# Value rows turned on their way to DRAM, first weights in halves, and a planner that counts the issuing queue as busy

## Chip, core and metric

One core of a Trainium2 chip. The metric is the device time of one execution in microseconds (us). TensorE is called PE, VectorE DVE, ScalarE ACT, GpSimd POOL and SyncE SP. Nearly all transfers are issued by SP, in the order of its instructions.

## The reference, cut to what matters

One encoder layer over 512 tokens of 1024 features, in float32:

```python
proj = h @ w_in                                  # queries, keys and values of two mixers, A and B
o_a = windowed_gqa_sink(rope(qa), rope(ka), va)  # 16 query heads, 4 key heads, |i-j| <= 128, blocks of 128
o_b = dilated_mixture(rope(qb), rope(kb), vb)    # 3 groups of 4 heads, dilation 1, 4, 16
g_a, g_b = split(sigmoid(h @ w_gate + b_gate))
y = (g_a * (o_a @ w_br_a) + g_b * (o_b @ w_br_b)) @ w_out
h = layer_norm(ALPHA * h + y)
f = (silu(h @ w_ff_gate) * (h @ w_ff_up)) @ w_ff_down
h = layer_norm(ALPHA * h + f)
```

## The kernel before

**Products.** Tokens stand in the order of four residues: token 4i + r is row i of residue r. Every float32 operand is split into a high part h and a low part l (a cast, then a subtraction), and a product is made of three: high by high, high by low, low by high. A *unit* of weights is 128 x 1024, loaded in two halves of 128 x 512 (256 KB); a half needs a staging slot ("ws", six of them) and two slots for its parts ("whl", sixteen). Lines 454 to 456 make the three products of one block of 128 features (`feat_k`), line 354 and line 333 the split of weights, and line 627 to 629 the values.

**The first units.** The first three units are `k`, `q` and `r` (keys of two heads, and queries). Their first halves come in two pieces, of `CUTS`, so that PE can begin early; `half_unit_by` loads, casts and subtracts each piece (lines 374 to 384). The eight blocks of x come from line 427, with the cast of line 429 and the subtraction of line 430. `FIRST` holds the priorities of these loads. Then, for each of the eight blocks, PE makes the three products of k, those of q and those of r.

**The order.** `ORDER` lists the work of the token mixers: `q2` is a unit of queries, `VA` the values of A and of B's first group, `T` a rotation of the heads gathered so far (rows are moved together by small transfers at line 483, turned on DVE, and moved back at line 504), `G` a gate unit, `A0` the attention of a group of heads in four blocks (`unit_a`), `B0` a head of mixer B (`unit_b`).

**The planner.** All operations are gathered with reads, writes and a priority: the PE time counted so far, plus an offset (-130 for weight loads and their splits, `EV` = -100 for what follows a product, `LATER` = 30). `Program.run` then goes through the operations with costs for each engine, picks for each free engine the ready operation of the lowest priority, and writes the instructions in this order. So the order on each engine is fixed when the program is built, and an engine waits where an operation in its list is not ready, whatever stands behind it. For SP, the planner counts an issue as 0.06 us and lets a backlog of issues grow beside it (`dma[0]`): a transfer that is ready is accepted at once.

**The values.** `token_values(False)` makes the values of A (256 columns) and of B's first group (256 columns) for the four residues. They are wanted by blocks of neighbouring tokens, so that rows have to be permuted: each residue's 128 x 512 is copied out of the accumulator and written to DRAM as it stands (line 639, one transfer of 256 KB). When all four are there, four transfers read A's blocks (line 645), 32 rows of each of the four residues, and eight read B's, shifted by half a block, 16 rows of each residue (line 651). `value_split` then makes a high and a low part of each block and group (a cast by line 333 or 335, a subtraction by line 589). The planner adds `READ` = 4 us to such a read.

**Where values are needed.** `unit_a` makes scores (lines 576, 577), exponentials on ACT (line 730), scaled probabilities (line 666 on ACT, 668 on DVE), transposes on PE (line 678) and then the products with the values (lines 743, 744).

Of the kernel before, what the change touches and what calls it, by code (L numbers as in the profile page):

```python
# [57 lines left out]
D_BANK = "s"  # L58
SPIN = 4

CUTS = ((0, 128), (128, 512))
FIRST = {("k", 0): (-1000, -998.3), ("q", 0): (-999.7, -998.1), ("r", 0): (-999.6, -998),
         ("k", 1): (-997.5,), ("q", 1): (-997.3,), ("r", 1): (-997.2,),
         "x": (-999.9, -998.4, -997.9, -997.8, -997.4, -997, -996.9, -996.8)}
N_WS, N_WHL, N_ATT, N_WHL1, N_TWO = 6, 16, 16, 40, 4


# [4 lines left out]


ORDER = """
q2 VA T G q3 A0 q4 G k1 T A1 q5 G q6 q7 T A2 G G A3
Q00 K00 T V Q02 K02 T Q01 K01 T B0 B1 G g Q10 K10 T g Q12 K12 T Q11 K11 T B2 B3 g8
"""

# [19 lines left out]
class Program:  # L98
# [72 lines left out]
    def run(self):  # L171
        engines = (PE, ACT, DVE, POOL, SP)
        free = {e: 0.0 for e in engines}
        pending = {e: [] for e in engines}
        times = [0.0]
        frees = []
        dma = [0.0, 0.0]

        def add(o):
            heapq.heappush(times, o.ready)  # L180
            for e, _ in o.alts:
                pending[e].append(o)

        seen = set()
        self.line, self.weights, self.loads = deque(), deque(), deque()
        for o in self.ops:
            new = [b for b in o.bufs if "gen" in b.keys and b not in seen]
            if new:
                seen.update(new)
                self.line.append(o)  # L190
            if o.strict and any("ws" in b.keys and b not in seen for b in o.bufs):
                seen.update(o.bufs)
                self.loads.append(o)
            if o.strict and any("whl" in b.keys and b not in seen for b in o.bufs):
                seen.update(o.bufs)
                self.weights.append(o)
            if o.left == 0:
                add(o)
        n_left = len(self.ops)
        while n_left:  # L200
            if not times:
                self.stuck(pending)
            now = heapq.heappop(times)
            while times and times[0] <= now:
                heapq.heappop(times)
            while frees and frees[0][0] <= now:
                _, _, b = heapq.heappop(frees)
                for key in b.keys:
                    if key in self.limits:
                        self.used[key] -= 1  # L210
            progress = True
            while progress:
                progress = False
                for e in engines:
                    if free[e] > now:
                        continue
                    best = None
                    for o in pending[e]:
                        if o.ready <= now and (best is None or o.prio < best.prio) and self.fits(o):
                            if e == DVE and len(o.alts) > 1 and free[ACT] < now + BIAS:  # L220
                                continue
                            best = o
                    if best is None:
                        continue
                    o = best
                    cost = dict(o.alts)[e]
                    if not o.urgent and any(q.urgent and now < q.ready < now + cost and q.prio < o.prio
                                            for q in pending[e]):
                        continue
                    for a, _ in o.alts:  # L230
                        pending[a].remove(o)
                    for b in o.bufs:
                        if b.tile is None:
                            b.tile = b.make()
                            for key in b.keys:
                                if key in self.limits:
                                    self.used[key] += 1
                    o.fn(e)
                    o.eng = e
                    if e == SP:  # L240
                        end = now + 0.06
                        dma[0] = max(dma[0], now) + (0.45 if cost > 0.2 else 0.62)
                        dma[1] = max(dma[1], dma[0] + 0.65) + cost
                        o.done = dma[1] + 0.9 + o.moves
                    elif o.moves:
                        end = now + cost
                        dma[1] = max(dma[1], end) + o.moves
                        o.done = dma[1] + 2.0
                    else:
                        end = now + cost  # L250
                        o.done = end
                    free[e] = end
                    heapq.heappush(times, end)
                    for b in o.bufs:
                        b.users -= 1
                        b.end = max(b.end, o.done)
                        if b.users == 0:
                            heapq.heappush(frees, (b.end + HOP, id(b), b))
                            heapq.heappush(times, b.end + HOP)
                    for q in o.succ:  # L260
                        same = len(q.alts) == 1 and q.alts[0][0] == e and e != SP and not o.moves
                        hop = SAME * (e in (ACT, DVE)) if same else HOP_PE if q.alts[0][0] == PE else HOP
                        q.ready = max(q.ready, o.done + hop)
                        q.left -= 1
                        if q.left == 0:
                            add(q)
                    n_left -= 1
                    progress = True
# [15 lines left out]
def pe(n):  # L284
    return max(0.11, 0.0133 + n / 2400)
# [3 lines left out]
def hybrid_layer(ctx: ExitStack, tc: tile.TileContext, wpack, xT, xtok, sink, bgate,  # L289
# [174 lines left out]
        for k in range(KD):  # L464
            feat_k(ps, wu, k, XM, xtok_of)

    EV, NOW, LATER, READ = -100.0, -300.0, 30.0, 4.0


    SHUF = [*range(8, 16), *range(0, 8), *range(24, 32), *range(16, 24)]  # L470
# [126 lines left out]
    def token_values(dilated):  # L597
# [22 lines left out]
        for r in range(NR):  # L620
            ps = bank("dense")
            for k in range(KD):
                wh, wl = parts_[k]

                def go(e, ps=ps, k=k, wh=wh, wl=wl, r=r):
                    a, b = xh[k]()[:, r * P:(r + 1) * P], xl[k]()[:, r * P:(r + 1) * P]
                    mm(ps.t, a, wh.t, start=(k == 0), stop=False)
                    mm(ps.t, a, wl.t, start=False, stop=False)
                    mm(ps.t, b, wh.t, start=False, stop=(k == KD - 1))

                op([(PE, 3 * pe(S))], go, reads=[wh, wl, *xtok_of(k)], writes=[ps])
                pr.T += 3 * pe(S)
            if dilated:
                for g in range(2):
                    res[g].append(value_split(ps, 256 * g, [ps]))
            else:
                t = slot()
                op(cp_alts(S, True), lambda e, t=t, ps=ps: copy(e, t.t, ps.t), reads=[ps], writes=[t], prio=EV)
                op([(SP, 0.73)], lambda e, t=t, r=r: nc.sync.dma_start(aside.t[r], t.t), reads=[t], writes=[(aside, r)],
                   prio=EV)  # L640
        if not dilated:
            raw = [slot() for _ in range(NR)]
            every = [(aside, r) for r in range(NR)]
            for m, t in enumerate(raw):
                op([(SP, 0.6)], lambda e, t=t, m=m: nc.sync.dma_start(
                    t.t[:, 0:256], aside.t[:, 32 * m:32 * m + 32, 0:256]), reads=every, writes=[(t, 0)], prio=EV, moves=READ)

            for m, t in enumerate(raw):
                for h in range(2):
                    c = 16 * ((2 * m - 1 + h) % 8)  # L650
                    op([(SP, 0.75)], lambda e, t=t, h=h, c=c: nc.sync.dma_start(
                        t.t[64 * h:64 * h + 64, 256:512], aside.t[:, c:c + 16, 256:512]), reads=every, writes=[(t, 1, h)],
                       prio=LATER, moves=READ)
            for g in range(2):
                for m, t in enumerate(raw):
                    res[g].append(value_split(t, 256 * g, [(t, 1, h) for h in range(2)] if g else [(t, 0)],
                                              LATER if g else EV))
        return res


# [277 lines left out]

    psk, psq, psr = bank("dense"), bank("dense"), bank("dense")
    for k in range(KD):  # L940
        for w, ps in (("k", psk), ("q", psq), ("r", psr)):
            feat_k(ps, [first[w, 0], first[w, 1]], k, XM, xtok_of)
    env = {"gate": 0, "qs": {}, "ks": {}, "turn": Turn()}
    ka = env["turn"].add(psk, k_post, 4)
    qa = env["turn"].add(psq, q_post, 4, (0, 0)) + env["turn"].add(psr, q_post, 4, (0, 0))
# [652 lines left out]
```

## Time and profile before

| | |
|---|---|
| median of 3 runs | 783.96 us (783.23 to 784.75) |
| profiled execution | 784.13 us, of which the span of instructions is 782.3 us |
| granted clock of PE | 0.996 |
| instructions | 13384, of which 4470 are products and as many weight loads |
| DMA | 113.36 MB, mean 145 GB/s |

The span is the time from the first to the last instruction; the rest of the profiled execution's time lies around it. A row of the timeline gives start, duration, engine, line, operation, output and input, shape and count; in square brackets stands how long the engine had been idle and what ended that. SPq rows are transfers at the moment at which SP issues them, not when they land. A PE row's duration reaches into the next one, since products are pipelined: the distance of two starts tells the pace.

### The profile page before, as it was taken

Reading aid. Unit: us, or ns where it says so; the run is one execution under the profiler, and the core shown is the slowest. Engines: PE = TensorE matmul, PEld = TensorE weight load, DVE = VectorE, ACT = ScalarE, POOL = GpSimd, SP = SyncE. Lnnn points to the kernel's source line nnn. Section 1 sums busy time; section 2 is a strip of 40 time slices with the busy share of each in tenths; the row PEclk is TensorE's granted clock in tenths of the full one; section 3 lists DMA queues with packets and bytes.
Section 4 is the critical chain, followed back from the end, with each engine's and each line's share of the span. In section 5 each row is a group of like instructions: output and inputs, shape, how many; then the busy total and the mean of one; then the engine's idle time right before and its main releaser. Section 6 shows DMA issues by size and latency. Waiting matters only on the chain.

```text
span 782.3 us, 13384 instructions
## 1 busy us (share of the span) xinstructions
PE 768.7 (98%) x4470; PEld 675.3 (86%) x4470; DVE 648.1 (83%) x1363; ACT 483.3 (62%) x1067; POOL 126.3 (16%) x288
## 2 busy tenths in 40 slices
PE   9998999999999999999999999999999999999995
PEld 5876888888888888888888899999999999999985
DVE  5486899888899899697687999888888889888697
ACT  5355796877688778693352667555665566555631
POOL 0010100101003503400011020142102330123002
PEclk9999999999999999999999999999999999999998
DMA  8745222312123324254373388689867986789202
GB/s 259 225 133 173 97 82 63 120 51 95 61 83 95 114 74 155 92 192 148 122 229 67 94 234 228 160 176 206 229 186 162 234 191 198 182 215 209 53 1 108
DMA packets 68789, 113.36 MB, mean 145 GB/s; under 512 B 8560, under 2 KB 17008, under 8 KB 68720
## 3 DMA queue, kind: packets, MB, share of 16 engines
q1 hardware_dynamic: 57056, 91.47, 36.1%
q0 software_dynamic: 11520, 20.98, 16.4%
q8 instruction: 35, 0.57, 0.3%
q14 instruction: 34, 0.28, 0.1%
q10 hardware_dynamic: 144, 0.07, 0.0%
HBM read 104.87 MB, written 4.72 MB: 140 GB/s over the span
## 4 chain that ended last, share of the span: by engine, by line
PE 89%; DMA 2%; DVE 1%; SPq 1%; issue 0%; ACT 0%; DVEq 0%; ACTq 0%
PE ps L454 10%; PE ps L455 10%; PE ps L456 10%; PE ps L1312 9%; PE ps L1311 9%; PE ps L1310 9%; PE ps L1439 4%; PE ps L1440 4%; PE ps L1441 4%; PE ps L1077 3%; PE ps L1076 3%; PE ps L1075 3%; PE ps L678 3%; PE ps L577 1%; PE ps L576 1%; PE ps L744 1%
## 5 line engine op out<-in xcount | busy, mean ns | idle before, releaser
L333 ACT ACTIVATE sl<-sl 128x512 fp32r<-128x512 f32 (+4 forms) x452 | 245.4, 570 | 87.7 <-PE ps L455 24.0
L1194 DVE TENSOR_TENSOR sl<-sl,sl 128x512 fp32r<-128x512 f32 (+3 forms) x304 | 169.9, 603 | 11.5 <-ACT sl L333 7.6
L333 ACT ACTIVATE sl<-ps 128x256 f32<-128x256 f32 (+4 forms) x204 | 89.4, 455 | 105.5 <-PE ps L1312 67.0
L454 PE MATMUL ps<-x,sl 128*128 128x512 f32 x304 | 121.4, 399 | 1.1 <-ACT sl L333 0.9
L455 PE MATMUL ps<-x,sl 128*128 128x512 f32 x304 | 119.3, 392 | 0.3 <-DVE x L430 0.2
L456 PE MATMUL ps<-x,sl 128*128 128x512 f32 x304 | 118.9, 391 | 0.4 <-DVE sl L354 0.4
L1264 POOL DMA_DIRECT2D sl<-wpack x44 | 40.4, 995 | 264.8 <-ACT sl L333 136.0
L354 DVE TENSOR_TENSOR sl<-sl,sl 128x512 fp32r<-128x512 f32 x114 | 75.7, 687 | 8.9 <-ACT sl L333 8.1
L1310 PE MATMUL ps<-x,sl 128*128 128x256 f32 x264 | 74.8, 283 | 0.0
L1312 PE MATMUL ps<-x,sl 128*128 128x256 f32 x264 | 74.7, 283 | 0.0
L1311 PE MATMUL ps<-x,sl 128*128 128x256 f32 x264 | 74.7, 283 | 0.0
L456 PEld LDWEIGHTS ps<-x,sl 128*128 128x128 f32 x304 | 57.1, 188 | 13.5 <-DVE sl L354 0.8
L1194 DVE TENSOR_TENSOR sl<-sl,ps 128x512 f32<-128x512 f32 (+1 forms) x78 | 47.4, 611 | 25.5 <-PE ps L1312 16.6
L454 PEld LDWEIGHTS ps<-x,sl 128*128 128x128 f32 x304 | 57.3, 189 | 11.9 <-ACT sl L333 2.2
L455 PEld LDWEIGHTS ps<-x,sl 128*128 128x128 f32 x304 | 57.3, 188 | 10.2 <-DVE x L430 1.2
L1311 PEld LDWEIGHTS ps<-x,sl 128*128 128x128 f32 x264 | 50.6, 192 | 0.5
L1310 PEld LDWEIGHTS ps<-x,sl 128*128 128x128 f32 x264 | 50.6, 192 | 0.5
L1312 PEld LDWEIGHTS ps<-x,sl 128*128 128x128 f32 x264 | 50.6, 192 | 0.0
L1312 PE MATMUL ps<-tw,sl 128*128 128x256 f32 x176 | 49.8, 283 | 0.0
L1311 PE MATMUL ps<-tw,sl 128*128 128x256 f32 x176 | 49.8, 283 | 0.0
L1312 PE MATMUL ps<-sl,sl 128*128 128x256 f32 x176 | 49.8, 283 | 0.0
L1310 PE MATMUL ps<-tw,sl 128*128 128x256 f32 x176 | 49.8, 283 | 0.0
(150 smaller groups left out, 1860.9 us busy)
## 6 DMA issues: line engine op xcount, KB each, us to landing
sl<-wpack SPq DMA_DIRECT2D x235, 256.0 KB
sl<-wpack POOLq DMA_DIRECT2D x44, 256.0 KB, 5.4
wf<-wpack SPq DMA_DIRECT2D x36, 256.0 KB
wf<-wpack POOLq DMA_DIRECT2D x36, 256.0 KB, 6.5
sl<-sl SPq DMA_DIRECT2D x88, 32.0 KB
sl<-xT SPq DMA_DIRECT2D x8, 256.0 KB
sl<-wpack SPq DMA_DIRECT2D x16, 128.0 KB
sl<-xtok SPq DMA_DIRECT2D x8, 256.0 KB
```

The costliest lines, as they stand in the source:

```text
L333: nc.scalar.activation(dst, src, AF.Copy)
L354: op([(DVE, dve(S))], lambda e: nc.vector.tensor_tensor(l.t, src.t, f32(h.t), op=ALU.subtract), reads=[src, h], writes=[l], prio=prio, abs ...
L454: mm(o, a, x0, start=(k == 0), stop=False)
L455: mm(o, a, x1, start=False, stop=False)
L456: mm(o, b, x0, start=False, stop=(k == nk - 1))
L1194: op([(DVE, dve(w))], lambda e: nc.vector.tensor_tensor(dst(), x(), y(), op=o), reads=reads, writes=writes, prio=prio)
L1264: return op([(POOL, 1.0)], lambda e: nc.gpsimd.dma_start(dst.t, wpack[u, :, j * S:(j + 1) * S], accum_op=ALU.add), reads=[dst], writes=[ds ...
L1310: mm(o, wh, bh[k](), start=(first and k == 0), stop=False, skip_group_check=True)
L1311: mm(o, wh, bl[k](), start=False, stop=False, skip_group_check=True)
L1312: mm(o, wl, bh[k](), start=False, stop=(k == 3), skip_group_check=True)
L1439: mm(ps.t, x0, w[0].t, start=(first and m == 0), stop=False, skip_group_check=True)
L1440: mm(ps.t, x0, w[1].t, start=False, stop=False, skip_group_check=True)
```

## The change

1. The first halves of k, q and r are cut into 256 and 256 columns instead of 128 and 384, and the priorities are set anew, so that x blocks 2 and 3 come ahead of some of the second pieces.
2. For each of the first six blocks, PE makes the products by parts: high by high for k, q and r, then low weight by high x for all three, then high weight by low x. For the last two blocks it finishes one unit after the other, in the same order of parts.
3. In `ORDER`, `k1` and `q6` each go ahead of a gate unit.
4. In the planner, SP is busy for the whole of an issue (0.45 or 0.62 us), so that it takes the most urgent ready transfer when it comes free.
5. Each residue's values are written by three transfers that put the rows where they are wanted (128 x 256, 112 x 256 and 16 x 256), and the blocks are read back by four transfers of 128 x 512. `READ` is 8 us.

```diff
-CUTS = ((0, 128), (128, 512))
-FIRST = {("k", 0): (-1000, -998.3), ("q", 0): (-999.7, -998.1), ("r", 0): (-999.6, -998),
-         ("k", 1): (-997.5,), ("q", 1): (-997.3,), ("r", 1): (-997.2,),
-         "x": (-999.9, -998.4, -997.9, -997.8, -997.4, -997, -996.9, -996.8)}
+CUTS = ((0, 256), (256, 512))
+FIRST = {("k", 0): (-1000, -998.4), ("q", 0): (-999.7, -998.2), ("r", 0): (-999.6, -998.1),
+         ("k", 1): (-997.7,), ("q", 1): (-997.5,), ("r", 1): (-997.4,),
+         "x": (-999.9, -998.5, -998.3, -998, -997.6, -997.3, -997.2, -997.1)}
...
-q2 VA T G q3 A0 q4 G k1 T A1 q5 G q6 q7 T A2 G G A3
+q2 VA T G q3 A0 q4 k1 G T A1 q5 q6 G q7 T A2 G G A3
...
                     if e == SP:
-                        end = now + 0.06
-                        dma[0] = max(dma[0], now) + (0.45 if cost > 0.2 else 0.62)
+                        end = now + (0.45 if cost > 0.2 else 0.62)
+                        dma[0] = end
...
-    EV, NOW, LATER, READ = -100.0, -300.0, 30.0, 4.0
+    EV, NOW, LATER, READ = -100.0, -300.0, 30.0, 8.0
...
-                op([(SP, 0.73)], lambda e, t=t, r=r: nc.sync.dma_start(aside.t[r], t.t), reads=[t], writes=[(aside, r)],
-                   prio=EV)
+                blocks = lambda r=r: aside.t[:, 32 * r:32 * r + 32, 0:256]
+                shifted = lambda a, b, r=r: aside.t.rearrange(
+                    "m (h q i) c -> (m h) q i c", h=2, q=4)[a:b, r, :, 256:512]
+                for n, (to, a, b, c) in enumerate(((blocks, 0, P, 0), (lambda v=shifted: v(1, 8), 0, 112, 256),
+                                                   (lambda v=shifted: v(0, 1), 112, P, 256))):
+                    op([(SP, 0.5)], lambda e, t=t, to=to, a=a, b=b, c=c: nc.sync.dma_start(to(), t.t[a:b, c:c + 256]),
+                       reads=[t], writes=[(aside, r, n)], prio=EV)
...
-            every = [(aside, r) for r in range(NR)]
             for m, t in enumerate(raw):
-                op([(SP, 0.6)], lambda e, t=t, m=m: nc.sync.dma_start(
-                    t.t[:, 0:256], aside.t[:, 32 * m:32 * m + 32, 0:256]), reads=every, writes=[(t, 0)], prio=EV, moves=READ)
-
-            for m, t in enumerate(raw):
-                for h in range(2):
-                    c = 16 * ((2 * m - 1 + h) % 8)
-                    op([(SP, 0.75)], lambda e, t=t, h=h, c=c: nc.sync.dma_start(
-                        t.t[64 * h:64 * h + 64, 256:512], aside.t[:, c:c + 16, 256:512]), reads=every, writes=[(t, 1, h)],
-                       prio=LATER, moves=READ)
+                op([(SP, 0.73)], lambda e, t=t, m=m: nc.sync.dma_start(t.t, aside.t[m]),
+                   reads=[(aside, r, n) for r in range(NR) for n in range(3)], writes=[t], prio=EV, moves=READ)
...
     for k in range(KD):
-        for w, ps in (("k", psk), ("q", psq), ("r", psr)):
-            feat_k(ps, [first[w, 0], first[w, 1]], k, XM, xtok_of)
+        parts, ws = ((0, 0), (1, 0), (0, 1)), (("k", psk), ("q", psq), ("r", psr))
+        for (wp, xp), (w, ps) in ([(p, w) for p in parts for w in ws] if k < 6 else [(p, w) for w in ws for p in parts]):
+            wt, c = first[w, k // 4][wp], (k % 4) * P
+            op([(PE, pe(S))], lambda e, ps=ps, wt=wt, c=c, xp=xp, k=k, wp=wp: mm(
+                ps.t, wt.t[:, c:c + P], (xh, xl)[xp][k](), start=(k == 0 and not wp and not xp),
+                stop=(k == KD - 1 and xp == 1)), reads=[wtok(wt, c), xtok_of(k)[xp]], writes=[ps])
+            pr.T += pe(S)
```

More of the change, by code (lines that the diff above doesn't have):

```diff
@@ L638, in token_values @@
                 op(cp_alts(S, True), lambda e, t=t, ps=ps: copy(e, t.t, ps.t), reads=[ps], writes=[t], prio=EV)
-                op([(SP, 0.73)], lambda e, t=t, r=r: nc.sync.dma_start(aside.t[r], t.t), reads=[t], writes=[(aside, r)],
-                   prio=EV)
+                blocks = lambda r=r: aside.t[:, 32 * r:32 * r + 32, 0:256]
[5 more added lines that the diff above has]
+                       reads=[t], writes=[(aside, r, n)], prio=EV)
         if not dilated:
             raw = [slot() for _ in range(NR)]
-            every = [(aside, r) for r in range(NR)]
             for m, t in enumerate(raw):
-                op([(SP, 0.6)], lambda e, t=t, m=m: nc.sync.dma_start(
-                    t.t[:, 0:256], aside.t[:, 32 * m:32 * m + 32, 0:256]), reads=every, writes=[(t, 0)], prio=EV, moves=READ)
-            for m, t in enumerate(raw):
-                for h in range(2):
-                    c = 16 * ((2 * m - 1 + h) % 8)
-                    op([(SP, 0.75)], lambda e, t=t, h=h, c=c: nc.sync.dma_start(
-                        t.t[64 * h:64 * h + 64, 256:512], aside.t[:, c:c + 16, 256:512]), reads=every, writes=[(t, 1, h)],
-                       prio=LATER, moves=READ)
+                op([(SP, 0.73)], lambda e, t=t, m=m: nc.sync.dma_start(t.t, aside.t[m]),
+                   reads=[(aside, r, n) for r in range(NR) for n in range(3)], writes=[t], prio=EV, moves=READ)
             for g in range(2):
                 for m, t in enumerate(raw):
-                    res[g].append(value_split(t, 256 * g, [(t, 1, h) for h in range(2)] if g else [(t, 0)],
-                                              LATER if g else EV))
+                    res[g].append(value_split(t, 256 * g, [t], LATER if g else EV))
         return res
```

## The prediction

> **What bounds the kernel now.** I read the page's busy totals first, then busy time by stretch, then the timelines of the three places where TensorE (PE) pauses.
>
> ```profile
> PE 768.7 (98%) x4470; PEld 675.3 (86%) x4470; DVE 648.1 (83%) x1363; ACT 483.3 (62%) x1067; POOL 126.3 (16%) x288
> ...
> 0.00:20.00 20.00, 18.31 (x67) 12.08 (x68) 10.47 (x21) 9.89 (x17) 0.20 (x4) 1.00 0.85 261
> 20.00:40.00 20.00, 20.00 (x90) 16.57 (x89) 8.59 (x15) 7.79 (x13) 0.00 (x0) 1.00 0.72 213
> 40.00:60.00 20.00, 18.67 (x82) 14.82 (x81) 15.68 (x27) 12.27 (x21) 3.53 (x8) 1.00 0.46 146
> 60.00:80.00 20.00, 17.46 (x84) 13.87 (x83) 13.38 (x39) 12.46 (x34) 1.67 (x8) 1.00 0.50 157
> 80.00:300.00 220.00, 220.00 (x1137) 187.29 (x1136) 196.23 (x492) 169.03 (x404) 30.99 (x121) 1.00 0.28 86
> 300.00:700.00 400.00, 399.88 (x2563) 363.64 (x2562) 338.00 (x653) 235.87 (x504) 76.02 (x133) 1.00 0.68 177
> 700.00:782.00 82.00, 74.41 (x458) 67.01 (x456) 65.75 (x122) 36.03 (x77) 13.86 (x14) 0.97 0.39 101
> ```
>
> Each row gives the stretch, its length, then busy PE, weight loads, DVE, ACT, POOL, granted clock, DMA share and GB/s. PE is the bound: from 80 to 700 us it is busy for 619.88 of 620 us. The same products run after the change, so time can only come out of PE's pauses: 1.69 us before 20, 1.33 in 40 to 60, 2.54 in 60 to 80, and 7.59 in the last stretch, which the change does not name. What is saved ahead of 80 us is kept if DVE follows: it has 23.77 us free in 80 to 300.
>
> **The first units.** PE rows, the casts that feed them, and one DVE row for later:
>
> ```profile
> 4.35 0.78 PE L454 MATMUL ps<-x,sl 128*128 128x512 f32 x1
> 5.25 0.50 PE L455 MATMUL ps<-x,sl 128*128 128x512 f32 x1
> 5.58 0.40 PE L456 MATMUL ps<-x,sl 128*128 128x512 f32 x1
> 5.82 0.40 PE L454 MATMUL ps<-x,sl 128*128 128x512 f32 x1
> ...
> 10.19 0.51 PE L454 MATMUL ps<-x,sl 128*128 128x512 f32 x1
> ...
> 12.87 0.40 PE L454 MATMUL ps<-x,sl 128*128 128x512 f32 x1
> ...
> 23.07 0.39 PE L454 MATMUL ps<-x,sl 128*128 128x512 f32 x1
> ...
> 28.52 0.39 PE L627 MATMUL ps<-sl,x 128*128 128x512 f32 x1
> ...
> 3.96 0.51 ACT L333 ACTIVATE sl<-sl 128x128 fp32r<-128x128 f32 x2 [1.49 <-DMA sl<-wpack]
> 4.97 0.31 ACT L333 ACTIVATE sl<-sl 128x128 fp32r<-128x128 f32 x1 [0.51 <-DMA sl<-wpack]
> 6.26 0.63 ACT L333 ACTIVATE x<-sl 128x512 fp32r<-128x512 f32 x1 [0.98 <-DMA sl<-xT]
> ...
> 9.50 1.30 ACT L333 ACTIVATE x<-sl 128x512 fp32r<-128x512 f32 x2 [0.73 <-DMA sl<-xT]
> ...
> 21.75 1.40 DVE L354 TENSOR_TENSOR sl<-sl,sl 128x512 fp32r<-128x512 f32 x2 [1.72 <-ACT sl L333]
> ...
> 66.60 0.42 ACT L333 ACTIVATE sl<-sl 128x256 fp32r<-128x256 f32 x1 [5.24 <-DMA sl<-va]
> ```
>
> The 72 products of k, q, r go from 4.35 to 23.07 = 18.72 us. The next 24, for q2, go from 23.07 to 28.52, which is 0.227 each; 72 at that pitch are 16.3, so 2.4 us are lost here. The rows show where: 4.35 to 5.25 (the low part of x is late), and the third block (10.19), which waits for the x cast of 9.50.
>
> Step by step. The first piece of each of three weights doubles to 128 KB: 64 KB more at 261 GB/s is 0.25 us, and the cast goes from 0.31 to 0.42 us, so the first product moves from 4.35 to about 4.7. The third weight's piece has 3 x 0.25 us more ahead of it: its cast of 4.97 becomes 5.7, done at 6.15. By parts, PE has k and q high products before that, r's at 6.15, and then six products that wait for nothing: block 0 ends near 7.75, where it ended near 7.2. Block 1 needs x1: 6.26 plus 0.75 is 7.0, cast by 7.65. The larger piece already holds its weights, so its nine products run from 7.75 to 9.8. Block 2's x lands behind 1280 KB instead of 1536 KB: 256 KB less is 1.0 us, so its cast moves from 9.50 to 8.5 and is done by 9.15; block 2 starts at 9.8 and ends at 11.85. Before, it started at 10.19 and, ended at 12.87. So **the start gains 1.0 us**. From block 3 on, the bytes ahead of each x are the same as before and PE is the slower side.
>
> The count of transfers, casts and subtractions is the same (two pieces before, two after), so the split itself costs nothing. Nor does going from bank to bank for each product: 5.58 to 5.82 is such a change of bank and takes 0.24. Each product loads its own weights already (4470 loads for 4470 products). The cover behind this block is q2's weights: their low parts come from 21.75 on, 0.70 us each, and PE would now want q2 at 22.05 and its third product at 22.5, just after 22.45. Loads of q2 now compete by priority with the tables that sit ahead of them in the queue, so I put that at zero; without it, it costs up to 0.7.
>
> **SP busy with each issue, and the two words moved.** These change the list that the planner writes, not any instruction. What the trace shows of the present list near 50 us:
>
> ```profile
> 50.05 0.39 PE L629 MATMUL ps<-sl,x 128*128 128x512 f32 x1
> 51.36 0.50 PE L454 MATMUL ps<-x,sl 128*128 128x512 f32 x1 [0.92 <-ACT sl L333]
> 51.70 0.40 PE L455 MATMUL ps<-x,sl 128*128 128x512 f32 x1
> 52.50 0.50 PE L456 MATMUL ps<-x,sl 128*128 128x512 f32 x1 [0.41 <-DVE sl L354]
> ...
> 34.01 1.14 SPq L483 DMA_DIRECT2D sl<-sl  x2
> ...
> 44.18 1.28 ACT L333 ACTIVATE sl<-sl 64x512 fp32r<-64x512 f32 x2 [9.43 <-DMA sl<-sl]
> ...
> 50.67 3.24 ACT L333 ACTIVATE sl<-sl 128x512 fp32r<-128x512 f32 x6
> ```
>
> PE loses 1.31 - 0.23 at 50.05 and 0.80 - 0.23 at 51.70: 1.65 us, for weights that are cast only at 50.67. ACT stood for 9.43 us before 44.18, waiting for a head rotation, and had the casts behind it. The rotation's last moves left at 34.01, behind weight loads that the old model had accepted the moment they were free. With a queue that is busy for each issue, the more urgent op is taken when the queue comes free, so these moves pass some loads: the bounds are nothing, and the whole loss: with 0.57 for an issue (1.14 for two), passing four loads makes 2.3 us. I take half the loss, **0.85 us**, because the moves also wait for the bytes in front of them, which the model's change doesn't remove. If the tables cos and sin fell late by the same rule, the rotation would wait for them; they rank at -95, its own moves at about -80, so they leave before these: nothing. Moving k1 and q6 ahead of a gate shifts 24 products each past 24 others; PE's sum stays, and A1 and A2, which they feed, lie past 80 where PE doesn't wait: nothing.
>
> **The value rows.** The rows for the way out, back, and what ACT did meanwhile:
>
> ```profile
> 56.09 0.33 SPq L639 DMA_DIRECT2D va<-sl  x1
> ...
> 61.10 2.33 SPq L645 DMA_DIRECT2D sl<-va  x4
> ...
> 63.99 6.87 SPq L651 DMA_DIRECT2D sl<-va  x8
> ...
> 71.61 3.66 SPq L341 DMA_DIRECT2D sl<-wpack  x5
> ...
> 69.54 0.42 ACT L333 ACTIVATE sl<-sl 128x256 fp32r<-128x256 f32 x1 [1.06 <-DMA sl<-va]
> 69.86 0.50 ACT L730 ACTIVATE sl<-sl,st 128x257 f32<-128x257 f32 x1
> ...
> ACT sl L333 <- DMA sl<-va: 7.5, 4, 5.2
> ...
> 71.85 0.40 PE L456 MATMUL ps<-x,sl 128*128 128x512 f32 x1
> 74.58 1.56 PE L678 MATMUL ps<-ident,sl 128*128 128x128 f32 x8 [2.34 <-ACT sl L666]
> ...
> 78.20 0.23 PE ps L743
> ...
> 66.80:71.30 4.50, 4.37 (x22) 3.41 (x21) 2.57 (x10) 2.39 (x7) 0.37 (x2) 1.00 0.27 91
> ```
>
> PE loses 2.73 - 0.23 = 2.5 us before the transposes at 74.58. They wait for probabilities, these for exponentials on ACT (69.86), and these stood behind value casts that waited 7.5 us for the reads. The reads themselves crawl: 91 GB/s with a DMA share of 0.27, some 4.3 of 16 engines. SP, too, is held: eight issues take 6.87 us and the next weights leave only at 71.61.
>
> After: 16 transfers as before, but 12 are writes. Of the last row, three writes instead of one: two more issues at 0.58 us (2.33 over 4) are 1.2. The new writes' views cut rows to 1 KB in the way that the slow reads do; that is not shown for a write, so its bounds are the old write's pace (nothing more) and 256 KB at 91 GB/s = 2.9 us, 1.9 more than at 261. I take the upper one, since its row is the nearest. The way out goes from 61.10 - 56.09 = 5.0 to 8.1 us. The reads back are plain rows: 1 MB at the 261 GB/s of the first row is 4.0 us, plus some 2.5 until the first begins to land (old casts of 66.60 and 69.54 are two apart, 1.5 each, so the first came near 65.1, 4.0 after its issue, of which 1.5 is its own transfer). So all values are back 8.1 + 6.5 = 14.6 us after the first of the last writes, against 69.54 - 56.09 = 13.5 for the first half alone before. The first half gains nothing; the second half and SP's queue do. What removes the stall is the doubled wait in the plan: the casts stand some 4 us later in ACT's list, behind exponentials, and ACT doesn't stand for them. What is late next is A0's product with the values: it stood at 78.20 and gets its values near 56.1 + 14.6 + 0.9 = 71.6, so it has slack. **I take the whole 2.5 us.** Nine of the writes, and their waits for the copies, lie under products for which everything is loaded (20 to 40 us: PE 20.00 of 20).
>
> [...]
>
> **Sum.** 784.13 (the profiled execution: span 782.3 and 1.83 around it, 0.17 above the median of 783.96) - 1.0 - 0.85 - 2.5 = **779.8 us**.
>
> **The rivals.**
> (1) The value rows come back too late anyway, since the slow pace is only moved to the writes: the stall of 2.5 stays or comes at the product with the values. For it: 0.27 DMA share; against: 6 us of slack at 78. Only 1.85 is gained: 782.3.
> (2) The gain is given back: PE arrives 1 us earlier at 50 and waits that much longer for the same casts (their slots come free with PE, but ACT's 9.43 us wait isn't PE's), and the stall at 74 only changes its cause. 784.
> (3) Slower: the list is drawn anew from the start to the end, and in the attention stretch PE's transposes stand behind softmax steps once per unit, as at 71.85. DVE is 89% busy there (196.23 of 220). Each costs 2.5; with 4.35 saved it decides from the third stall on (4.35 + 1.6 = 5.9): with three, 784.13 - 4.35 + 7.5 = 787.3. Against it: today's list has one stall of this size in 20 units (four groups of four A blocks, four B heads).
> (4) All pauses go, 2.4 + 1.65 + 2.5, and some fractions beside them: 777.
>
> **How the numbers follow.** Forecast 0.58 (778 to 782), rival (1) 0.14, (2) 0.13, (3) 0.10, (4) 0.05. A measurement of this kernel can tell about 0.2%, 1.6 us: the line between faster and same is 782.4. Faster: 0.58 + 0.05 + most of (1), 0.11 = 0.74; same: the rest of (1) and (2) = 0.16; slower 0.10. For 8 in 10 the range goes from (4), 776.8, to (2), 784.0; the forecast's own is 778 to 782.
>
> **What would show it.** Right: three products of different banks in a row from 4.7, block 2 at about 9.8, q2 near 22; after PE's last value product a pause under 1 us; 12 writes and four reads of 256 KB, each landing within 1 us of the one before, and a DMA share near 0.9 while they run; no ACT wait for the read of over 1 us; PE over 19.5 of 20 in 60 to 80. Wrong: a PE wait of over 1 us for transposes or values anywhere between 60 and 330, or rotation moves that leave later than 34.

## The result, and the profile after

The changed kernel takes 779.75 us (median of 6 runs, 779.47 to 781.3) against 784.56 us before (6 runs, 783.23 to 785.62): a ratio of 0.9943, with a 95% interval of 0.9929 to 0.9957. The forecast was 779.8. The number was met, but not by the terms that were added up to it, as the parts below show.

Busy time by stretch of the kernel after, with the columns as before (length, PE, weight loads, DVE, ACT, POOL, clock, DMA share, GB/s), and then all waits of PE (us in total, times, longest; line 409 is a warm-up ahead of the first product):

```profile
0.00:20.00 20.00, 17.55 (x67) 12.36 (x68) 13.02 (x24) 12.20 (x21) 0.20 (x4) 1.00 0.88 276
40.00:60.00 20.00, 20.00 (x90) 16.57 (x89) 14.34 (x24) 13.32 (x23) 3.44 (x8) 1.00 0.53 157
60.00:80.00 20.00, 20.00 (x105) 17.26 (x104) 18.13 (x51) 15.55 (x43) 2.60 (x8) 1.00 0.49 167
80.00:300.00 220.00, 220.00 (x1132) 186.89 (x1131) 199.21 (x501) 168.09 (x397) 27.30 (x121) 1.00 0.29 91
300.00:700.00 400.00, 398.96 (x2571) 363.71 (x2570) 337.81 (x646) 232.58 (x495) 77.03 (x137) 1.00 0.68 175
...
PE ps L941 <- ACT sl L333: 1.2, 1, 1.2
PE ps L409 <- DVE eps L441: 1.2, 1, 1.2
PE ps L675 <- ACT sl L663: 0.9, 1, 0.9
```

Both pauses of 40 to 80 us are gone: 20.00 of 20 where 18.67 and 17.46 stood. In the first 20 us PE stands longer (it is busy for 17.55 us instead of 18.31), yet the products that follow come no later, as the next rows show. A new pause opens at 327.6, where transposes wait for ACT: 0.9 us in the row of line 675 above, 1.1 from start to start. The timelines of the places that the prediction named, PE first, then DVE, ACT and SP (in the kernel after, line 941 makes the first products, 645 the value writes, 650 the reads, 663 and 675 are the old 666 and 678):

```profile
4.82 0.92 PE L941 MATMUL ps<-x,sl 128*128 128x512 f32 x2
6.96 2.57 PE L941 MATMUL ps<-x,sl 128*128 128x512 f32 x10 [1.23 <-ACT sl L333]
22.97 0.39 PE L454 MATMUL ps<-x,sl 128*128 128x512 f32 x1
28.41 0.39 PE L627 MATMUL ps<-sl,x 128*128 128x512 f32 x1
49.94 0.39 PE L629 MATMUL ps<-sl,x 128*128 128x512 f32 x1
50.17 0.39 PE L454 MATMUL ps<-x,sl 128*128 128x512 f32 x1
...
36.98 0.73 DVE L494 STREAM_SHUFFLE sl<-sl 128x512 f32<-128x512 f32 x1
...
6.49 0.42 ACT L333 ACTIVATE sl<-sl 128x256 fp32r<-128x256 f32 x1 [1.43 <-DMA sl<-wpack]
48.31 3.24 ACT L333 ACTIVATE sl<-sl 128x512 fp32r<-128x512 f32 x6
66.69 0.40 ACT L333 ACTIVATE sl<-sl 128x256 fp32r<-128x256 f32 x1
...
31.17 1.53 SPq L341 DMA_DIRECT2D sl<-wpack  x3
32.80 1.14 SPq L483 DMA_DIRECT2D sl<-sl  x2
...
53.95 2.13 SPq L645 DMA_DIRECT2D va<-sl  x3
61.25 1.75 SPq L650 DMA_DIRECT2D sl<-va  x4
DMA to landing us min/median/max: 2.9/3.1/4.5
```

At 5.3 us PE stands for the third weight's piece, cast at 6.49. The last value product at 49.94 is followed by the next unit at once, because its weights' casts begin at 48.31 instead of 50.67, because the rotation's shuffle begins at 36.98. The value casts on ACT (66.69) show no wait for the reads. The last three writes leave from 53.95, the four reads from 61.25 to 63.0. The landing times of the last row are of writes and reads together; each of the four reads took 3.1 us.

### The profile page after: what moved, and what is told of

Its sections match the earlier page's. It is cut to its first block, busy times and chain, and to the rows that moved or that the text cites. A ratio compares the mean times of both kernels' runs of the same rounds, so it can differ in the third digit from the quotient of the medians.

```text
span 777.9 us, 13378 instructions
## 1 busy us (share of the span) xinstructions
PE 766.2 (99%) x4470; PEld 675.9 (87%) x4470; DVE 652.7 (84%) x1373; ACT 479.7 (62%) x1057; POOL 122.2 (16%) x288
## 4 chain that ended last, share of the span: by engine, by line
PE 96%; DVE 1%; ACT 1%; DMA 1%; issue 0%; SPq 0%; DVEq 0%; ACTq 0%
PE ps L454 10%; PE ps L455 10%; PE ps L456 10%; PE ps L1314 9%; PE ps L1313 9%; PE ps L1312 9%; PE ps L1441 4%; PE ps L1442 4%; PE ps L1443 4%; PE ps L675 3%; PE ps L1077 3%; PE ps L1079 3%; PE ps L1078 3%; PE ps L941 2%; PE ps L627 2%; PE ps L629 2%
## 5 line engine op out<-in xcount | busy, mean ns | idle before, releaser
L333 ACT ACTIVATE sl<-sl 128x512 fp32r<-128x512 f32 (+4 forms) x456 | 247.9, 571 | 79.7 <-DMA sl<-wpack 20.4
L333 ACT ACTIVATE sl<-ps 128x256 f32<-128x256 f32 (+4 forms) x188 | 81.6, 450 | 106.3 <-PE ps L1314 65.6
L454 PE MATMUL ps<-x,sl 128*128 128x512 f32 x280 | 110.9, 396 | 0.0
L455 PE MATMUL ps<-x,sl 128*128 128x512 f32 x280 | 109.5, 391 | 0.0
L456 PE MATMUL ps<-x,sl 128*128 128x512 f32 x280 | 109.3, 390 | 0.0
L456 PEld LDWEIGHTS ps<-x,sl 128*128 128x128 f32 x280 | 52.6, 188 | 11.5
L454 PEld LDWEIGHTS ps<-x,sl 128*128 128x128 f32 x280 | 52.7, 188 | 8.5
L455 PEld LDWEIGHTS ps<-x,sl 128*128 128x128 f32 x280 | 52.7, 188 | 8.3
L1313 PEld LDWEIGHTS ps<-x,sl 128*128 128x128 f32 x264 | 50.6, 192 | 0.5
L1312 PEld LDWEIGHTS ps<-x,sl 128*128 128x128 f32 x264 | 50.6, 192 | 0.5
L1314 PEld LDWEIGHTS ps<-x,sl 128*128 128x128 f32 x264 | 50.6, 192 | 0.0
L1314 PE MATMUL ps<-tw,sl 128*128 128x256 f32 x176 | 49.8, 283 | 0.0
L1313 PE MATMUL ps<-tw,sl 128*128 128x256 f32 x176 | 49.8, 283 | 0.0
L1314 PE MATMUL ps<-sl,sl 128*128 128x256 f32 x176 | 49.8, 283 | 0.0
L1313 PE MATMUL ps<-sl,sl 128*128 128x256 f32 x176 | 49.8, 283 | 0.0
```

The lines of the kernel that those rows point to most:

```text
L333: nc.scalar.activation(dst, src, AF.Copy)
L454: mm(o, a, x0, start=(k == 0), stop=False)
L455: mm(o, a, x1, start=False, stop=False)
L456: mm(o, b, x0, start=False, stop=(k == nk - 1))
L1312: mm(o, wh, bh[k](), start=(first and k == 0), stop=False, skip_group_check=True)
L1313: mm(o, wh, bl[k](), start=False, stop=False, skip_group_check=True)
```

## The experiments

Ratios are to the kernel before on the same chip, with 95% intervals. Each pause below is a distance of two PE starts, less the pitch of the row before it (0.23 us for a product of 512 columns; for a transpose of 128 columns 0.06, an estimate at a quarter of that). Eight transposes go from 92.50 to 93.30 in the kernel before, 0.10 each; with this the pauses behind a transpose, 0.8 us at 71.12 in experiment 3 and 1.1 at 328, are 0.04 shorter. Line numbers shift a little from kernel to kernel: the low parts of A's attention outputs stand at line 996 in the kernel before and at 993, 998 or 1001 in others.

**1. The longer wait for reads, alone.**

```diff
-    EV, NOW, LATER, READ = -100.0, -300.0, 30.0, 4.0
+    EV, NOW, LATER, READ = -100.0, -300.0, 30.0, 8.0
```

> The kernel before with READ = 8 instead of 4 in the planner, and nothing else. Theory (the planner's longer wait moves the value casts behind the exponentials on ACT, so that ACT does not stand for the reads): the pause before the first transposes near 72 to 75 us (2.5 us) goes, the one near 50 us (1.65) stays; 2 to 3 us faster. Rival (plain reads of 2 KB rows are what ends the stall): the reads still take 12 us, the pause stays or moves to the product with the values; within 1 us of before.

Measured: 1.0035 (1.0022 to 1.0049), slower, where 2 to 3 us faster was expected. The stretch of 60 to 80 us, one at the end of the attention with the waits of PE there, and DVE's rows:

```profile
60.00:80.00 20.00, 20.00 (x105) 17.28 (x104) 16.16 (x47) 14.83 (x39) 1.90 (x8) 1.00 0.53 170
...
340.00:350.00 10.00, 6.56 (x24) 5.04 (x23) 9.68 (x17) 8.07 (x16) 0.00 (x0) 0.87 0.31 105
...
PE ps L455 <- DVE sl L996: 3.4, 1, 3.4
...
339.28 0.69 DVE L996 TENSOR_TENSOR sl<-tw,sl 128x512 fp32r<-128x512 f32 x1
340.56 5.50 DVE L354 TENSOR_TENSOR sl<-sl,sl 128x512 fp32r<-128x512 f32 x9
345.98 3.09 DVE L996 TENSOR_TENSOR sl<-tw,sl 128x512 fp32r<-128x512 f32 x5
```

The pause before the transposes is gone with this one constant, and the reads are still the old twelve: the first half of the theory holds. But the time is given back at 343 us, a place that neither theory had. There PE begins the branch units and needs the low parts of A's attention outputs (line 996), and five of the eight stand on DVE behind nine weight splits (line 354). Those become possible all at once when the planner raises its limit of weight slots at the end of the attention, and they rank ahead (-130 to -20). PE waits 3.4 us (3.6 from start to start), and the granted clock is 0.87 over that stretch. In the kernel before, four of A's low parts stand just ahead of the nine splits:

```profile
339.72 1.29 DVE L996 TENSOR_TENSOR sl<-tw,sl 128x512 fp32r<-128x512 f32 x2
343.25 0.69 DVE L996 TENSOR_TENSOR sl<-tw,sl 128x512 fp32r<-128x512 f32 x1
344.68 0.69 DVE L996 TENSOR_TENSOR sl<-tw,sl 128x512 fp32r<-128x512 f32 x1
345.96 5.54 DVE L354 TENSOR_TENSOR sl<-sl,sl 128x512 fp32r<-128x512 f32 x9
```

In the kernel after, all but two of the eight are done by then (one row below holds two of them):

```profile
341.53 1.29 DVE L998 TENSOR_TENSOR sl<-tw,sl 128x512 fp32r<-128x512 f32 x2
343.08 5.50 DVE L354 TENSOR_TENSOR sl<-sl,sl 128x512 fp32r<-128x512 f32 x9
348.50 0.68 DVE L998 TENSOR_TENSOR sl<-tw,sl 128x512 fp32r<-128x512 f32 x1
```

Neither has a pause there: enough of them are ready when PE comes to them. The count of low parts ahead of that run of splits orders the pauses of all kernels with the old priority: with six or five ahead (the kernels after and before) there is none, with four (experiments 3 and 8, ten splits in the run) it is 2.75 us, with three (1, 2 and 4) 3.6, and with two (7) 1.5 and 4.5.

**2. The writes and plain reads, alone.** The hunk of `token_values`, with `READ` = 4.

> The kernel before with the twelve writes and four plain reads, READ = 4, nothing else. Theory: the first half of the values comes back no sooner (about 14 us after the first of the last writes), ACT still stands for it, and the pause near 72 stays at 2 to 3 us; within 1 us of before, or up to 1 slower. Rival: values come back in under 9 us, the pause is gone; 2 to 3 us faster.

Measured: 1.0064 (1.004 to 1.0088), slower by 4.5 us, where at most 1 us was expected. Waits of this kernel:

```profile
ACT sl L333 <- DMA sl<-va: 5.6, 3, 4.5
PE ps L675 <- ACT sl L663: 1.8, 1, 1.8
PE ps L455 <- DVE sl L993: 3.4, 1, 3.4
```

ACT still stands 4.5 us for the first read and PE 1.8 us for the transposes. The rival falls: plain reads don't end that stall. The rest of the loss is again the pause behind the nine splits, here 3.6 us at 346.6.

**3. SP busy with each issue, alone.**

```diff
-                        end = now + 0.06
-                        dma[0] = max(dma[0], now) + (0.45 if cost > 0.2 else 0.62)
+                        end = now + (0.45 if cost > 0.2 else 0.62)
+                        dma[0] = end
```

> The kernel before with SP busy for each issue in the planner, nothing else. Theory (the rotation's moves pass the weight loads, so the rotation lands about 2 us sooner and the casts of the next weights follow sooner): the pause near 50 us (1.65) goes to under 0.5, the one near 72 stays; 1 to 2 us faster. Rival (the pause near 50 went because of the new first units or the order of k1): the pause near 50 stays; within 0.5 of before.

Measured: 1.0045 (1.0028 to 1.0062), slower, where 1 to 2 us faster was expected.

```profile
36.63 0.73 DVE L494 STREAM_SHUFFLE sl<-sl 128x512 f32<-128x512 f32 x1
...
69.23 0.39 PE L456 MATMUL ps<-x,sl 128*128 128x512 f32 x1
71.12 0.30 PE L678 MATMUL ps<-ident,sl 128*128 128x128 f32 x1 [1.51 <-ACT sl L730]
71.95 1.94 PE L678 MATMUL ps<-ident,sl 128*128 128x128 f32 x7 [0.53 <-ACT sl L666]
...
71.00:76.00 5.00, 4.35 (x15) 3.52 (x16) 4.71 (x15) 4.77 (x13) 0.00 (x0) 0.66 0.64 200
```

The place is as expected: the shuffle begins at 36.63, and there is no pause near 50. The pause before the transposes stays, the granted clock over 71 to 76 is now 0.66, and a pause of 2.75 us opens at 348.4.

The pause near 50 hangs on that shuffle, the first step of the head rotation once its last moves have landed. In every profile the unit after the values begins 12.0 us after the shuffle, or right behind the last value product where that comes later. The five kernels in which PE waits show it:

| kernel | shuffle begins | next unit begins | difference | pause |
|---|---|---|---|---|
| before | 39.34 | 51.36 | 12.02 | 1.1 |
| experiment 2 | 38.86 | 50.88 | 12.02 | 1.0 |
| experiment 7 | 37.88 | 49.88 | 12.00 | 0.4 |
| experiment 9 | 39.92 | 51.91 | 11.99 | 2.0 |
| experiment 12 | 38.54 | 50.55 | 12.01 | 1.7 |

Each of these five has another 0.6 us at the unit's third product. The kernel before and experiments 1 and 9 have the same list up to there, and in them the shuffle begins at 39.34, 37.89 and 39.92: a single profile of such a list doesn't say whether the pause is there. That experiment 1 had none is chance, then, and not its edit. In the seven kernels without the busy SP (before, 1, 2, 4, 7, 9, 12) the shuffle begins at 37.88 to 39.92; in the seven with it (after, 3, 5, 6, 8, 10, 11) at 36.63 to 37.77, ahead of all of those, and the next unit follows the last value product at the pitch in each (three of them stand 0.4 to 0.7 us at its third product). So the busy SP does bring the rotation sooner.

How it does so is not the step that the theory named. In all fourteen lists SP issues the same 46 other transfers, 31 of them weights, ahead of the rotation's last two moves: these pass no weight load. What the list changes is where the loads stand. With the busy SP the tables cos and sin leave later and half of the sixteen loads of line 610 sooner, and three weight loads instead of four stand directly ahead of the last moves (31.17 and 32.80 in the rows of the kernel after). In the kernel before, the four and then the moves at 34.01:

```profile
31.91 2.00 SPq L341 DMA_DIRECT2D sl<-wpack  x4
```

With the busy SP the last moves are issued at 32.5 to 33.7 and the shuffle begins 4.1 to 4.5 us after that; without it they are issued at 33.2 to 34.9, and the shuffle begins 4.4 to 5.3 us after. Which of the changes in the order does this was not tried.

**4. The first units in halves and by parts, alone.** The hunks of `CUTS`, `FIRST` and the first products.

> The kernel before with the first units in halves, their new priorities and the products by parts, nothing else. Theory (the third weight's larger piece comes late and takes back what the parts win): the first value product moves by less than 0.5 us from 28.5; pauses near 50 and 72 stay; within 0.7 us of before. Rival (the gain of 1.0 us is there once nothing else is changed): first value product near 27.5, 1 us faster.

Measured: 1.015 (1.0114 to 1.0186), the slowest. The pauses are 0.8 us at 70.9, 2.0 at 238.5 and 3.6 at 349.4: the list as a whole is drawn anew by an edit to its first 20 us. The first value product came at 29.9, against the theory's "less than 0.5 us from 28.5". In this profile PE's 33 products from 6.70 take 9.55 us, 0.29 each, where in the kernel after the 22 from 6.96 take 5.29, 0.24 each: over 33 products this alone is some 1.6 us. Here are its longest waits:

```profile
PE ps L455 <- DVE sl L1001: 3.4, 1, 3.4
PE ps L803 <- ACT sl L333: 1.8, 1, 1.8
PE ps L944 <- ACT sl L333: 0.7, 1, 0.7
```

**5 to 8. The changed kernel, less one part each.** Each takes back the hunk of one part (5 the start, 6 the value rows, 7 the busy SP, 8 the moved words).

> The changed kernel with the first units as before (pieces of 128 and 384, three products at a time). Theory (the new start won 0.1 us, by PE's first value product): 779 to 781, the pauses near 50 and 72 stay away. Rival (the start's change moved the list so that the pause near 50 went): a pause of over 1 us near 50, 781 to 783.

> The changed kernel with the value rows as before (four writes, twelve reads), READ = 8. Theory (the plan's wait ended the pause near 72, not the plain reads): no pause of over 1 us before the first transposes, 779 to 781. Rival (the plain reads did): reads at about 91 GB/s take 12 us, a pause of 2 us or more between 65 and 85, 782 to 784.

> The changed kernel with SP's issues counted as 0.06 us in the planner, as before. Theory (the busy SP ended the pause near 50): a pause of 1 to 2 us near 50 is back; 781 to 782. Rival (the order of k1, the start or the writes did): no pause near 50; 779 to 780.5.

> The changed kernel with k1 and q6 behind the gate units, as before. Theory (the moved words do nothing for PE, since no pause hangs on them): 779 to 781, no new pause. Rival (k1's rotation ahead of the gate is what keeps ACT from standing near 72 to 80): a pause of 1 to 3 us between 60 and 110; 781 to 783.

| without | ratio | interval | pauses over 1 us after 28 us |
|---|---|---|---|
| 5, the start | 0.9951 | 0.9936 to 0.9966 | 1.1 at 328 |
| 6, the value rows | 0.9948 | 0.9931 to 0.9965 | 1.1 at 328 |
| 7, the busy SP | 1.0138 | 1.0123 to 1.0154 | 3.2 at 298, 1.5 at 346, 4.5 at 349 |
| 8, the moved words | 0.9985 | 0.9976 to 0.9995 | 2.8 at 345 |
| nothing (the kernel after) | 0.9943 | 0.9929 to 0.9957 | 1.1 at 328 |

Neither the start nor the value rows can be told from nothing. In 6 the reads are the old ones, 0.51 us and more for an issue as before, and ACT does not wait for them at all:

```profile
L651 SPq DMA_DIRECT2D sl<-va x8: 509/515/527, 60.4 to 68.8; - x8
...
60.00:80.00 20.00, 20.00 (x106) 17.18 (x105) 17.46 (x49) 14.45 (x39) 1.96 (x8) 1.00 0.55 163
```

Without the busy SP the kernel is 10.6 us slower than the one before and some 15 slower than the one after, where the theory had 1 to 2. Its pause near 50 is back with 0.4 and 0.6 us, less than the 1 to 2 expected; the largest pauses stand at the same place near 345 us. Without the moved words some 3 us are lost, and not near 70 as the rival had it, but again there.

**9 and 10. A's output splits ahead of the weight splits.** Experiments 1 and 8 with one number changed, so that the low parts no longer stand behind the nine weight splits:

```diff
-    sa = [split_of(lambda t=t, m=m: t.t[:, m], [(t, b) for b in range(NR)], -20) for t in oa2 for m in range(2)]
+    sa = [split_of(lambda t=t, m=m: t.t[:, m], [(t, b) for b in range(NR)], -200) for t in oa2 for m in range(2)]
```

> READ = 8 alone on the kernel before, as in the first experiment (0.35% slower than before), and the splits of A's attention outputs at priority -200 instead of -20, so that they stand ahead of the nine weight splits on ACT and DVE. Theory (the early pauses go, and are given back at 343 us because the outputs' low parts stand behind nine weight splits that become possible at once): no pause of over 1 us at 335 to 360, the clock stays at 1.00 there, and the gain shows: 779 to 781. Rival (ACT and DVE are simply full there, so the pause only moves): a pause of 2 us or more between 330 and 365 stays, 784 to 787.

> The changed kernel without the moved words k1 and q6 (783.4, with a pause of 2.75 us at 344.8 and a lower clock after it), and the splits of A's attention outputs at priority -200. Theory (the moved words matter only through where those splits fall at 345): no pause of over 1 us at 335 to 360, 779 to 780.5, as the changed kernel. Rival (the moved words matter by themselves): 782 to 784.

Measured: 0.9963 (0.9949 to 0.9977) for 9, where it was 1.0035, and 0.9932 (0.9916 to 0.9947) for 10, where it was 0.9985. Experiment 9 at the end of the attention, stretch and DVE:

```profile
340.00:350.00 10.00, 10.00 (x46) 8.28 (x45) 9.83 (x20) 8.22 (x17) 0.00 (x0) 1.00 0.46 160
...
341.40 3.09 DVE L996 TENSOR_TENSOR sl<-tw,sl 128x512 fp32r<-128x512 f32 x5
```

The five low parts stand at 341.40 instead of 345.98, PE doesn't pause, and DVE is just as full (9.83 of 10): it was the order, not DVE's load. So the wait for reads is worth its gain, which experiment 1 had lost again later, and no other use of the moved words can be told: without them and with this number, the kernel takes 779.12 us on a chip where the one before takes 784.47. It beats the kernel before clearly; against the kernel after (0.9943) the intervals overlap. The number alone, on the kernel before or on the kernel after, was not tried; neither has a pause at 345 for it to end.

**11. Small first pieces, products by parts.** The kernel after with `CUTS` of 128 and 384 columns.

> The changed kernel with the first pieces of 128 columns (and 384) and the rest as it is, products by parts too. Theory (the larger first piece of the third weight is what holds PE at 5.3 to 7.0): first product near 4.35, the pause of 1.6 us at 5.3 under 0.5, but the second pieces come later for block 1, so the first value product at 27.3 to 28.0; 778.5 to 780. Rival (the x blocks hold PE, not the pieces): the first value product within 0.2 of 28.4; same as the changed kernel.

```profile
4.34 3.67 PE L941 MATMUL ps<-x,sl 128*128 128x512 f32 x10
8.30 1.42 PE L941 MATMUL ps<-x,sl 128*128 128x512 f32 x5 [0.29 <-DVE sl L382]
...
5.08 0.31 ACT L333 ACTIVATE sl<-sl 128x128 fp32r<-128x128 f32 x1 [0.62 <-DMA sl<-wpack]
...
27.92 0.39 PE L627 MATMUL ps<-sl,x 128*128 128x512 f32 x1
```

The ratio is the same, 0.9943 (0.9928 to 0.9957). The third piece is cast at 5.08 for 6.49 and the pause at 5.3 is gone, so PE did stand for that piece in the profile of the kernel after. That it came late because it is larger doesn't follow: with the same larger pieces, experiments 6, 10 and 12 have all three cast by 5.33 and PE doesn't stand there. Experiment 6, ACT:

```profile
4.30 1.03 ACT L333 ACTIVATE sl<-sl 128x256 fp32r<-128x256 f32 x3 [1.84 <-DMA sl<-wpack]
```

The first value product is 0.5 us sooner than in the kernel after, as expected, and the whole is not measurably faster.

**12. Without the busy SP, and A's output splits ahead.** Experiment 7 with the number of 9.

> The changed kernel with SP's issues counted as 0.06 us (794.9, with pauses of 3.15 us at 298 and 1.45 and 4.52 at 345 to 349 and a lower clock after them), and the splits of A's attention outputs at priority -200. Theory (of its loss against the changed kernel, some 8 us between 345 and 360 come from where those splits fall, and the rest from SP's planned order): the pauses at 345 to 360 go, one of 2 to 4 us between 230 and 300 stays, 785 to 789. Rival 1 (all of the loss is where the splits fall): 779 to 781. Rival 2 (SP's planned order starves PE near 345 whatever the splits do): 792 to 796.

Measured: 1.0054 (1.0026 to 1.0081) where it was 1.0138. The pauses at 345 to 350 are gone, the one at 298 stays:

```profile
298.57 0.39 PE L456 MATMUL ps<-x,sl 128*128 128x512 f32 x1
301.89 1.01 PE L800 MATMUL ps<-sl,sl 128*128 128x256 f32 x4 [2.93 <-ACT sl L333]
```

So of the 15 us by which experiment 7 stands behind the kernel after, about 6.6 (1.0138 less 1.0054, of 784) came from where the low parts fall; both rivals fall. Among the rest are this pause, where scores of a B head wait for casts on ACT, a slower pace of PE behind it (the row at 302.69 lasts 0.63 us, those ahead of the pause 0.39), and pauses of 1.7 and 0.6 us near 50 and 0.7 near 237. Why the planner without a busy SP puts the list of 298 us that way was not tried.

## Why the prediction was right, point by point

- **The bound and the places.** Right in that PE is the bound and the named places hold most of the gain; between 80 and 300 PE is busy for 220 of 220 us in both. But busy time is too coarse to add up the gain: PE's idle time fell only by 1.9 us (782.3 - 768.7 = 13.6 before, 777.9 - 766.2 = 11.7 after), the span by 4.4, since a PE row's duration reaches into the next row (0.39 us at a pitch of 0.23) and hides a small gap. Starts are the better measure: the first product behind the branch units (line 1075, 1077 after) stands at 396.31 before and at 391.58 after, 4.7 us sooner, and PE's last product, too, is 4.7 us sooner.
- **The start, 1.0 us.** Not met in the profile of the kernel after: the first product came at 4.82 (4.7 forecast), but the third weight's piece was cast at 6.49, not 5.7, and q2 began at 22.97, not 22.05: 0.1 us gained. The term that failed here is the arrival of the third piece, and a fixed price for its bytes doesn't describe it: in the seven profiles with the larger pieces its cast came anywhere from about 5.0 (6, 10, 12) over 5.7 (7, 8) to 6.23 and 6.49 (4 and after). The first value product came at 27.1 to 27.8 in five of them, at 28.4 in the kernel after and at 29.9 in experiment 4; with the old start it came at 28.1 to 28.7. So the start is worth about 0.7 us between the medians, 1.0 is within what single executions show, and in the time it can't be told from nothing (experiment 5).
- **The pause near 50, 0.85 us.** Right that the busy SP ends it; wrong in the step and in the size. The moves were to pass weight loads, and they passed none: 46 transfers go ahead of the last moves in every list (experiment 3). All 1.65 us went, not half. Of the 2.4 us by which the shuffle began sooner (39.34 to 36.98) a part is chance, since it differs by 2.0 us between profiles of one list.
- **The pause at 72, 2.5 us.** Right, and by the mechanism named: the wait in the plan (experiments 1 and 6), not the reads (2). The way out took 61.25 - 53.95 = 7.3 us, between the two bounds for it (5.0 + 1.2 = 6.2, and 8.1), and the reads landed 3.1 us after their issue, so that all values were back near 65.7, some 12 us after the first of the last writes against 14.6.
- **The pace of the reads and of the writes.** The four plain reads of 128x512 landed 3.1 us after their issue each, where the old reads moved at 91 GB/s (66.8 to 71.3 in the kernel before). That the new writes go at the old reads' pace, as the prediction's upper bound has it, is the author's estimate, and no run here shows it: only writes of 16 KB have a landing on record (2.9 to 4.5 us), none of them among the last three, and the way out of 7.3 us lies between the bounds.
- **The moved words, nothing.** Wrong as a price: without them some 3 us are lost (experiment 8). Right only in that PE gains nothing by them in the stretch where they stand; they move the low parts at 345, as experiment 10 shows.
- **What the sum left out.** A new pause of 1.1 us at 328, and above all a place where many an edit of the list is paid: the run of weight splits at the end of the attention. Rival (3) had the right kind (PE waits in a list drawn anew, with a point from which it decides), in the wrong place, and gave it 0.10. The four parts that were tried alone are each slower than the kernel before, all with a pause there, and the fifth loses some 3 us there when it is left out. That the whole change doesn't is a property of its list that nothing in the profile before showed. The pause at 328, too, is of the kind that the prediction named as a sign of being wrong (PE waiting over 1 us for transposes between 60 and 330).
- **Why the number was met all the same.** By luck. The start gave 0.9 us less than its term, the pause near 50 gave 0.8 more, the pause at 328 cost 1.1, and 0.1 + 1.65 + 2.5 - 1.1 = 3.15 us is what these places make. By its starts PE gains 4.7 us ahead of 396 us, so 1.6 more lie in smaller gaps, which the sum put at nothing and which were not followed one by one; behind PE's last product 0.3 are lost again, and the span is 4.4 shorter.

## What to carry to other kernels

When a planner draws the whole list anew, the gain at the edited place is the easy part of the forecast; look for the places where many operations become possible at one moment (a raised limit, a freed pool) and ask what urgent work could fall behind them. An edit that is slower alone may be right: two lists can differ far from the edit, so compare the pauses, not only the totals, and repair the place where the gain is given back before judging the edit. And a pause that hangs on which of two times comes later can come and go between executions of the same list (near 50 us it was 1.1 us, none and 2.0 us in the kernel before and experiments 1 and 9, whose lists are the same up to there), so one profile is not enough to call it ended; the time of the operation that it hangs on, over several lists, is the better witness. Even then, count what the step in between is said to move: the transfers ahead of the last moves were the same 46 in every list.

## What the runs showed of the hardware

In some of these profiles a PE pause cost more than its length, since the products behind it came slower, at a lower granted clock. In experiment 3 a pause of 1.7 us ends at 71.12 and one of 0.8 us follows; from 71 to 76 the clock was 0.66, and two products behind the pauses (73.54 and 74.12) start 0.58 us apart instead of 0.23; in the kernel before, the clock was 1.00 from 71 to 80, around the single pause of 2.5 us at 71.85. In experiment 9 it was 0.50 from 52.8 to 56.2, with starts 0.43 us apart (54.07 and 54.50):

```profile
52.80:56.20 3.40, 3.15 (x7) 2.51 (x8) 3.40 (x7) 2.90 (x6) 0.24 (x1) 0.50 0.82 243
```

This stretch begins inside the second of two pauses, of 2.0 and 0.6 us, with two products between them. So pauses of about the same length in all were followed by different clocks; what decides that, no run here shows.
